# A two-level Strassen run that starts two items sooner in the third column, with one fetch less per item, another order of left forms, and the last results in halves

## The chip, the cores and the metric

The kernel runs on one core of one Trainium2 chip. The metric is the device time of one launch, in microseconds, as the median of several runs. Five engines work side by side, each in its own order: PE multiplies matrices (PEld is its loading of weights), DVE adds tensors, ACT copies and applies tanh, POOL and SP issue transfers from their queues. They wait for one another by semaphores.

## The reference

```python
def reference(a, b, bias):          # a: 4096x4096, b: 4096x4096, bias: 4096, all float32
    return np.tanh(np.matmul(a, b) + bias)
```

## The kernel before

**Tiles.** The output is worked in four columns of 1024 (c = 0 to 3). A row pair is 256 rows; there are 16. One *item* is a row pair in one column, and its work is one level of Strassen-Winograd: seven products instead of eight. The products are named m1 to m7 (`PRODUCTS`); each has a left operand (a quadrant of a such as a11, or a sum such as s2) and a right operand (a quadrant of b such as b11, or a sum such as d3, e6). Each operand is fp16. A whole product is 16 matmuls of 128x512 (line 478, or line 950 within the run described below).

**Two levels.** Two items side by side can be taken together, and a product of both can be split once more: seven products of 8 matmuls of 128x256 (line 889) in place of two whole ones. Their left operands are the *left forms* v1 to v4 (made on DVE into four tiles called h by `left`), besides two halves of the operand itself; their right operands are three quarters of the operand of b and the *right forms* t1 to t4. For m3 and m4 (and for m5 and m7 within a run) the right forms stay in SBUF; `resident` makes those of m5 and m7. For m2 and m6 they are written to DRAM once (`put_four` by way of a staging tile, `put_sum` by two transfers of which the second adds) and pulled again for each pair by `pull_four` on POOL. The five tiles that they are pulled into are blocks of b11 and e6; where another column follows, those blocks are saved in DRAM first (`put_block`) and brought back behind the run.

**Stages of columns 2 and 3.** Each starts with two half items that repeat the row pairs just done (`again`), so that the operands of b can be changed part by part (`change`). Then come pairs of *plain* items, where m3 and m4 go in two levels (`twice_four`) and m2, m5, m1, m6, m7 whole; then the *run*, `four(n)` for each pair, where m2 to m7 go in two levels and only m1 is whole. `FOURS` says how many plain items stand ahead of the run: 4 in column 2, 2 in column 3. The last pair of column 2 *leaves*: its m6 and m7 are whole, since b's operands are restored there for what follows. `turn_over(c)` writes out by hand the last part of the last plain pair and what it loads ahead for the run.

**Order.** The order of every queue is the order in which the program writes the instructions. Time is counted in slots, seven for an item; `at_slot` puts work at a slot. `STAGED`, `ASIDE`, `ADDED`, `SAVED`, `AWAY` and `KEPT_AT` give the slots for forms, counted from the second to last item before the run (slot -14 is the start of the column with two plain items, -28 with four). Lines 250, 258, 371 and 381 are loads of a and b; lines 776, 764, 783 and 790 are the writes of forms and blocks.

**The names that the steps touch.** a12 holds s5, the left operand of m5, and later s7, that of m7. `product` (line 483) fetches a12 of the item two on when it stands in `early_fetch`; `after` (line 573) fetches it when the item is one of a pair. `take_m5` (line 1033) takes the finished m5: it writes o from an output tile (three of them, lines 497 to 498), applies tanh, stores, and takes m5 from ds. Then m7 needs s7 (`asum`) and its v1, and m6 needs its v2. `last` marks the last pair of the program; its end is lines 1200 to 1218. `new_sum` gives a tile for a sum out of a pool of two (`sums`) or, at each third turn, a single spare tile, which the stages use too.

Of the kernel before, what the change touches and what calls it, by code (L numbers as in the profile page):

```python
# [8 lines left out]
P = 128  # L9
QP = 32  # L10
NB = 512
NCW = 2 * NB
# [8 lines left out]
ADD = mybir.AluOpType.add  # L21
# [47 lines left out]

FOUR = ((0, 0), "t1", (1, 0), "t2", "t3", (1, 1), "t4")  # L70
ADDED = {
    2: {("m2", "t3"): (-20, -18)},
    3: {("m2", "t3"): (-12, -10), ("m6", "t3"): (2, 5)},
}
STAGED = {2: (-13, -7, -5, 0, 2, 4, 7), 3: (-8, -6, -4, 1, 4, 7)}
ASIDE = {2: (-9, -10, -6, 2, 4, 5), 3: (-12, -7, -10, -2, 6, 4)}
SAVED = {2: (-13, -8, -13, 5, -5, -7, 5, 7)}
SPARED = (1,)
S6_AT = 2
AWAY = {"m5": -14, "m7": -3}  # L80
# [3 lines left out]
    ("m5", "t1"): -7, ("m5", "t3"): -6, ("m5", "t2"): -3, ("m5", "t4"): -1,  # L84
    ("m7", "t1"): -4, ("m7", "t2"): 0, ("m7", "t4"): 1, ("m7", "t3"): 2,
}
FOURS = {2: 4, 3: 2}

# [34 lines left out]
def kernel(  # L123
# [28 lines left out]
    def tt(out_, in0, in1, op):  # L152
        nc.vector.tensor_tensor(out=out_, in0=in0, in1=in1, op=op)  # L153
# [55 lines left out]
    def beginning(n):  # L209
        return begins.get(items[n][0], len(items))  # L210

    def by_two(n, what):
        return what in twos.get(n, ())

    def again(n):
        return items[n][3]
# [99 lines left out]

    def new_sum(shape, dt, name, n=None):
        pool = sums
        if n is None or not (by_two(n, "m6") or by_two(n - 2, "m6") or n in fours or items[n][0] in FOURS and (not again(n) or items[n][0] == NC - 1 and items[n][2] in SPARED) and n < beginning(n)):
            turns[0] += 1  # L320
            pool = spare if turns[0] % 3 == 0 else sums
        return pool.tile(shape, dt, name=name, tag="sum")
# [667 lines left out]
    def four(n):  # L990
# [17 lines left out]
            at = "w" if what == "m6" else "z"  # L1008
            whole(i, left_, right, ((bank(i, 0, at), ds(0, NB)),), what == "m6", steps)

        def store_half(o, i, j, queue):
            queue.dma_start(
                out=out[ds(2 * pair[i] * P, P), ds(c * NCW + HALF[j].start, HALF[j].size)],
                in_=o[:, HALF[j]],
            )

        def end(name, i, r, j):
            nc.scalar.activation(st[i][name], st[i][name], TANH)
            store(st[i][name], pair[i], r, c, j)
# [13 lines left out]
        def take_m5(i):  # L1033
            st[i]["o"] = new_out()
            tt(st[i]["o"], st[i]["s"], bank(i, 0, "d"), ADD)
            end("o", i, 0, 1)
            tt(st[i]["ds"], st[i]["ds"], bank(i, 0, "d"), SUB)

        def take_m1(i):
# [31 lines left out]
        step(2)  # L1071
        single(n, "m4", 7)
        w2()
        forms_at(1)
        left(n, "m3", "v4")
        u()
        single(n, "m3", 7)
        u2()
        seed(p, "z", 0)
# [48 lines left out]
            fetch(m + 1, "a22")  # L1128
        take_m2(q)
        take_m5(p)  # L1130
        seed(p, "d", 0)
        seed(q, "c", 0)
        asum(q, "s6")
# [5 lines left out]
        one_whole("m1", p)  # L1139
        take_m5(q)  # L1140
        if leave:
            asum(q, "s7")
            take_m1(p)
            if not last:
                fetch(m, "a11")
            for name in ("t1", "t2", "t4"):
                del rights["m5", name], rights["m7", name]
            step(11)
            one_whole("m1", q)
            take_m1(q)  # L1150
            step(12)
            for i in (p, q):
                one_whole("m6", i)
                step(14 if i == p else 16)
                take_m6(i)
                one_whole("m7", i)
                if i == p:
                    fetch(m, "a21")
                    fetch(m, "a12")
                    asum(m, "s2")  # L1160
                take_m7(i)
                step(15 if i == p else 17)
                if i == p:
                    for name in AHEAD[0]:
                        fetch(m + 1, name)
            for name in AHEAD[1]:
                fetch(m + 1, name)
            asum(m, "s5")
            for k in range(18, 29):
                at_slot(SLOTS * m + k - 18, give_back, c, k)  # L1170
            return
        left(n, "m6", "v2")
        group0(n, "m6")
        asum(q, "s7")
        left(n, "m7", "v1")
        take_m1(p)
        if not last:
            fetch(m, "a11")
# [19 lines left out]
        w2()  # L1198
        u()
        if last:  # L1200
            single(n, "m7", 7)
            u2()
            here = bank(q, 0, "d")[:, HALF[0]]
            tt(here, here, st[q]["ds"][:, HALF[0]], SUB)
            o = st[q]["ds"]
            tt(o[:, HALF[1]], o[:, HALF[1]], bank(q, 0, "d")[:, HALF[1]], SUB)
            nc.scalar.activation(o[:, HALF[1]], o[:, HALF[1]], TANH)
            store_half(o, q, 1, nc.sync)
            single(n, "m6", 3)
            take_m6(p)  # L1210
            single(n, "m6", 4)
            take_m6(q)
            single(n, "m7", 3)
            take_m7(p)
            single(n, "m7", 4)
            nc.scalar.activation(o[:, HALF[0]], here, TANH, scale=-1.0)
            store_half(o, q, 0, nc.sync)
            return
        single(n, "m7", 7)
        u2()  # L1220
# [41 lines left out]
    def turn_over(c):  # L1262

        m = begins[c]
        p, q = m - 2, m - 1
        left_count[0] = 0
        del free[:]

        def slot(at):
            for f, args in work.pop(SLOTS * p + at, ()):  # L1270
                if f in (put_four, put_sum, put_block):
                    f(*args)

        queue.extend(
            (what, f) for n in range(m, ends_with[c], 2) for what in ("m2", "m6") for f in FOUR
            if what == "m2" or n + 2 in fours or c == NC - 1
        )
        returned.clear()
        if c < NC - 1:
            returned.append(c)  # L1280
        early_fetch.update((m, m + 1))
        free.extend(("b11_1", "b11_2", "b11_3"))
        for i in range(3):
            pull_four()
        asum(q, "s1")
        asum(q, "s6")
        fetch(m, "a11")
        slot(8)
        product(p, *PRODUCTS[8])
        single(p, "m4", 7)  # L1290
        adds["m4"][1]()
        product(q, *PRODUCTS[2])
        resident_at(-7)
        single(p, "m4", 3)
        twice_after(p, "m4")
        twice_four(p, "m4", 3)
        fetch(m, "a22")
        fetch(m + 1, "a22")
        fetch(m + 1, "a11")
        asum(q, "s7")  # L1300
        slot(9)
        slot(10)
        seed(m, "d", 0)
        resident_at(-6)
        product(q, *PRODUCTS[5])
        fetch(m, "a21")
        slot(12)
        resident_at(-5)
        slot(13)
# [549 lines left out]
```

## Time and profile before

| | us |
|---|---|
| median of three runs | 1522.38 (1521.57 to 1523.24) |
| profiled execution, its own time | 1522.57 |
| its span, first to last instruction | 1520.6 |
| column 2's first product of line 889 | 838.77 |
| column 2's run, first m1 to the m1 of the pair that leaves | 954.46 to 1086.02 |
| column 3's first product of line 889 | 1207.15 |
| column 3's run, first m1 to the end of the span | 1277.02 to 1520.6 |

The granted PE clock is 1.0 throughout. How to read the rows that follow: in a timeline each row has the start, the duration, the engine, the line, the operation with output and inputs, shapes and a count, and in brackets the idle time of that engine ahead of it with what ended it. Rows of the same kind in sequence are merged. In the chain of waits each row is a start, a duration and what the program's end hung on at that time. In a table of windows the columns are the stretch, its length, busy time of PE, PEld, DVE, ACT and POOL (with counts), the clock, the share of the DMA engines and GB/s. A transfer's row ends with its count, size and the median time from issue to landing. DVE's adds all stand on line 153, and the scalar copies of PSUM on lines 895 to 908: both are helpers.

### The profile page before, as it was taken

What the parts mean: (1) busy time and instruction counts of PE and PEld (TensorE: products, weight loads), DVE (VectorE), ACT (ScalarE), POOL (GpSimd) and SP (SyncE); (2) the same over time, 40 slices, a digit from 0 to 9 for tenths busy, and PEclk for the clock granted to TensorE, in tenths of its full rate; (3) what the DMA queues carried; (4) which work ended last, traced back from release to release, by engine and by line L of the source; (5) the groups of instructions that cost most, each with busy time, mean ns of one, the idle gap of its engine ahead of it and who ended that gap; (6) DMA issues with size and microseconds to landing.
All of it is one profiled execution on the core that took longest, in us unless ns stands there. A gap on an engine that the chain in (4) does not pass through costs nothing.

```text
span 1520.6 us, 23784 instructions
## 1 busy us (share of the span) xinstructions
PE 1509.8 (99%) x9005; PEld 878.9 (58%) x9005; DVE 1166.8 (77%) x1619; ACT 377.1 (25%) x809; POOL 479.1 (32%) x868
## 2 busy tenths in 40 slices
PE   9999999999999999999999999999999999999998
PEld 4444444444445566544444557788644467888886
DVE  6789877777876666577787667888658868888887
ACT  4431111111221122111122212333222222333332
POOL 8775543333603231343460220112121121111111
PEclk9999999999999999999999999999999999999999
DMA  9999999999979998999995887898976688888885
GB/s 181 181 217 255 275 247 212 215 214 240 189 212 298 263 278 269 229 258 229 239 188 158 292 293 257 312 344 300 376 247 196 215 284 276 303 311 309 325 332 181
DMA packets 205718, 387.74 MB, mean 255 GB/s; under 512 B 25250, under 2 KB 102306, under 8 KB 205604
## 3 DMA queue, kind: packets, MB, share of 16 engines
q0 software_dynamic: 117232, 198.50, 56.8%
q1 hardware_dynamic: 87844, 187.47, 35.3%
q8 instruction: 70, 1.15, 0.3%
q14 instruction: 44, 0.36, 0.1%
q10 hardware_dynamic: 528, 0.26, 0.1%
HBM read 332.40 MB, written 139.46 MB: 310 GB/s over the span
## 4 chain that ended last, share of the span: by engine, by line
PE 91%; DMA 4%; DVE 3%; POOL 1%; issue 0%; ACT 0%; DVEq 0%; SPq 0%; ACTq 0%; POOLq 0%
PE ps L478 58%; PE ps L889 21%; PE ps L1488 4%; PE ps L950 4%; PE ps L678 4%; DMA a<-scratch 2%; DMA out_dram<-o 1%; DVE h L153 1%; DVE a L153 1%; DVE ps L153 0%; DMA land<-in_a_dram 0%; DVE ds L153 0%; DMA side<-in_b_dram 0%; POOL land L1529 0%; POOL side L1577 0%
## 5 line engine op out<-in xcount | busy, mean ns | idle before, releaser
L478 PEld LDWEIGHTS <-a 128*128 128x128 f16 x3264 | 319.2, 98 | 379.0 <-DMA a<-scratch 0.5
L478 PE MATMUL ps<-b,a 128*128 128x512 f16 x1148 | 262.1, 379 | 0.0
L889 PEld LDWEIGHTS <-h 128*128 128x128 f16 x2048 | 199.2, 98 | 31.8 <-DVE h L153 6.3
L478 PE MATMUL ps<-e,a 128*128 128x512 f16 x932 | 212.1, 379 | 0.0
L478 PE MATMUL ps<-d,a 128*128 128x512 f16 x896 | 202.5, 379 | 0.0
L827 POOL DMA_DIRECT2D form<-form_m x133 | 70.6, 531 | 378.4 <-PE ps L889 337.6
L278 DVE STREAM_TRANSPOSE a<-nat 128x1024 f16<-128x1024 f16 (+2 forms) x202 | 175.2, 911 | 19.1 <-PE ps L478 17.6
L889 PEld LDWEIGHTS <-a 128*128 128x128 f16 x1536 | 150.3, 98 | 24.0
L478 PE MATMUL ps<-d,s 128*128 128x512 f16 x656 | 148.3, 379 | 0.0
L478 PEld LDWEIGHTS <-s 128*128 128x128 f16 x848 | 83.0, 98 | 97.7
L250 POOL DMA_DIRECT2D nat<-in_a_dram x176 | 93.3, 535 | 133.6 <-DVE a L278 64.4
L381 POOL DMA_DIRECT2D b<-in_b_dram x192 | 103.7, 546 | 83.9 <-DVE a L278 30.9
L153 DVE TENSOR_TENSOR a<-a,a 128x2048 f16<-128x2048 f16 (+1 forms) x97 | 116.5, 1201 | 0.2
L153 DVE TENSOR_TENSOR ps<-ps,x 128x256 f32<-128x256 f32 x146 | 60.8, 429 | 60.2 <-ACT x L895 32.8
L889 PE MATMUL ps<-form,h 128*128 128x256 f16 x768 | 98.0, 273 | 2.5 <-DVE h L153 2.5
L502 ACT ACTIVATE o<-ps 128x512 f32<-128x512 f32 x90 | 54.1, 601 | 162.2 <-issue 105.9
L153 DVE TENSOR_TENSOR h<-a,h 128x1024 f16<-128x1024 f16 x128 | 86.7, 684 | 0.0
L889 PE MATMUL ps<-form,a 128*128 128x256 f16 x608 | 77.5, 273 | 0.0
L153 DVE TENSOR_TENSOR ds<-ds,ps 128x512 f32<-128x512 f32 (+1 forms) x94 | 63.6, 678 | 17.3 <-PE ps L889 7.0
L478 PE MATMUL ps<-side,a 128*128 128x512 f16 x288 | 73.9, 379 | 0.0
L950 PE MATMUL ps<-d,a 128*128 128x512 f16 x320 | 72.2, 379 | 0.0
L153 DVE TENSOR_TENSOR h<-a 128x1024 f16<-128x1024 f16 x80 | 54.7, 688 | 16.4 <-DMA a<-scratch 15.7
(187 smaller groups left out, 1874.2 us busy)
## 6 DMA issues: line engine op xcount, KB each, us to landing
a<-scratch SPq DMA_DIRECT2D x144, 512.0 KB, 6.4
form<-form_m POOLq DMA_DIRECT2D x133, 512.0 KB, 5.8
out_dram<-o SPq DMA_DIRECT2D x203, 256.0 KB, 5.5
nat<-in_a_dram POOLq DMA_DIRECT2D x288, 128.0 KB, 6.4
scratch<-a SPq DMA_DIRECT2D x48, 512.0 KB, 6.6
b<-in_b_dram POOLq DMA_DIRECT2D x160, 128.0 KB, 5.5
scratch<-a SPq DMA_DIRECT2D x32, 256.0 KB, 5.7
cast<-in_b_dram POOLq DMA_DIRECT2D x64, 128.0 KB, 10.0
```

Of the source, the lines that this page charges most:

```text
L153: nc.vector.tensor_tensor(out=out_, in0=in0, in1=in1, op=op)
L250: nc.gpsimd.dma_start(out=tl[ds(q * QP, QP), :, :], in_=src.rearrange("(mb p) k -> p mb k", p=QP),)
L278: nc.vector.transpose(dst[:, ds(b0 * tb, n * tb), :].rearrange("P (b t) (mb p) -> P mb b t p", t=tb, p=QP), src[:, :, ds(b0, n), :].rearra ...
L381: nc.gpsimd.dma_start(out=dst[ds(q * QP, QP), ds(t, nt)], in_=src)
L478: nc.tensor.matmul(st[where], at, bt, start=(what == "m2" or n < LEAD and what == "m1") and i == 0, stop=i == len(ts_) - 1, skip_group_che ...
L502: nc.scalar.activation(o, src, TANH)
L678: nc.tensor.matmul(to, at, bt, start=False, stop=t == TP - 1, skip_group_check=True)
L827: nc.gpsimd.dma_start(out=rights[what, name], in_=forms[what, name])
L889: nc.tensor.matmul(to, at, bt, start=False, stop=t == TP - 1, skip_group_check=True)
L950: nc.tensor.matmul(to[:, half], at[:, t // TB, t % TB], bop[right, t // TB][:, t % TB, half], start=anew and t == 0, stop=t == T - 1, skip ...
L1488: nc.tensor.matmul(mb[m % 4, j], aq[m, kt // T][:, kt % T, :], right(kt, j), start=fresh and kt == k0, stop=stop and kt == k1 - 1, skip_gr ...
```

## The change

Four edits.

1. **The run of column 2 starts two items sooner** (`FOURS` 4 to 2): items 33 and 34 go from the plain kind into the run, which then has five pairs in column 2 instead of four; column 3 has six in both. The slots of the forms of column 2 become those of column 3; m6's t3 is made by adding transfers there too; the saved blocks have new slots; and s1 of the second repeated item of column 2 takes the pool of two, as column 3's does.
2. **No second fetch of a12**: `turn_over` no longer puts the first two items of the run into `early_fetch`, so that line 483 doesn't fetch what line 573 fetches.
3. **Order in the run**: s7 and m7's v1 go ahead of m6's v2 and its first products; taking m5 from ds (`less_m5`) is its own step, and for the second item it goes behind them. One group of resident forms (m7's t4) is made behind m3's v4 and its add instead of ahead.
4. **The last pair**: m6 and m7 of the last item are both finished in halves, the second half of the columns first; the order of the last four products is m6, m7 of the first item, then m6, m7 of the second; the very last store goes out from ACT's queue.

```diff
 ADDED = {
-    2: {("m2", "t3"): (-20, -18)},
+    2: {("m2", "t3"): (-12, -10), ("m6", "t3"): (2, 5)},
...
-STAGED = {2: (-13, -7, -5, 0, 2, 4, 7), 3: (-8, -6, -4, 1, 4, 7)}
-ASIDE = {2: (-9, -10, -6, 2, 4, 5), 3: (-12, -7, -10, -2, 6, 4)}
-SAVED = {2: (-13, -8, -13, 5, -5, -7, 5, 7)}
+STAGED = {2: (-8, -6, -4, 1, 4, 7), 3: (-8, -6, -4, 1, 4, 7)}
+ASIDE = {2: (-12, -7, -10, -2, 6, 4), 3: (-12, -7, -10, -2, 6, 4)}
+SAVED = {2: (-16, -15, -11, -9, -14, -13, 0, 3)}
...
-FOURS = {2: 4, 3: 2}
+FOURS = {2: 2, 3: 2}
...
-  ... items[n][0] in FOURS and (not again(n) or items[n][0] == NC - 1 and items[n][2] in SPARED) and n < beginning(n)
+  ... items[n][0] in FOURS and (not again(n) or items[n][2] in SPARED) and n < beginning(n)
...
             end("o", i, 0, 1)
+
+        def less_m5(i):
             tt(st[i]["ds"], st[i]["ds"], bank(i, 0, "d"), SUB)
...
         w2()
-        forms_at(1)
         left(n, "m3", "v4")
         u()
+        forms_at(1)
...
         take_m5(p)
+        less_m5(p)
...
         take_m5(q)
         if leave:
+            less_m5(q)
...
+        asum(q, "s7")
+        left(n, "m7", "v1")
         left(n, "m6", "v2")
         group0(n, "m6")
-        asum(q, "s7")
-        left(n, "m7", "v1")
+        less_m5(q)
         take_m1(p)
...
         if last:
+            parts = {"m6": ("s", "w", ADD, 1.0, 1), "m7": ("ds", "d", SUB, -1.0, 0)}
+
+            def first_half(what):
+                name, at, op, scale, r = parts[what]
+                o, here = st[q][name], bank(q, 0, at)
+                tt(here[:, HALF[0]], here[:, HALF[0]], o[:, HALF[0]], op)
+                tt(o[:, HALF[1]], o[:, HALF[1]], here[:, HALF[1]], op)
+                nc.scalar.activation(o[:, HALF[1]], o[:, HALF[1]], TANH)
+                store_half(o, q, r, 1, nc.sync)
+
+            first_half("m6")
             single(n, "m7", 7)
             u2()
-            here = bank(q, 0, "d")[:, HALF[0]]
-            tt(here, here, st[q]["ds"][:, HALF[0]], SUB)
-            o = st[q]["ds"]
-            tt(o[:, HALF[1]], o[:, HALF[1]], bank(q, 0, "d")[:, HALF[1]], SUB)
-            nc.scalar.activation(o[:, HALF[1]], o[:, HALF[1]], TANH)
-            store_half(o, q, 1, nc.sync)
+            first_half("m7")
             single(n, "m6", 3)
             take_m6(p)
-            single(n, "m6", 4)
-            take_m6(q)
             single(n, "m7", 3)
             take_m7(p)
-            single(n, "m7", 4)
-            nc.scalar.activation(o[:, HALF[0]], here, TANH, scale=-1.0)
-            store_half(o, q, 0, nc.sync)
+            for what in ("m6", "m7"):
+                name, at, op, scale, r = parts[what]
+                single(n, what, 4)
+                o = st[q][name]
+                nc.scalar.activation(o[:, HALF[0]], bank(q, 0, at)[:, HALF[0]], TANH, scale=scale)
+                store_half(o, q, r, 0, nc.sync if what == "m6" else nc.scalar)
             return
...
-        early_fetch.update((m, m + 1))
```

More of the change, by code (lines that the diff above doesn't have):

```diff
@@ L318, in new_sum @@
         pool = sums
-        if n is None or not (by_two(n, "m6") or by_two(n - 2, "m6") or n in fours or items[n][0] in FOURS and (not again(n) or items[n][0] == NC - 1 and items[n][2] in SPARED) and n < beginning(n)):
+        if n is None or not (by_two(n, "m6") or by_two(n - 2, "m6") or n in fours or items[n][0] in FOURS and (not again(n) or items[n][2] in SPARED) and n < beginning(n)):
             turns[0] += 1
@@ L1009, in one_whole, with store_half @@
             whole(i, left_, right, ((bank(i, 0, at), ds(0, NB)),), what == "m6", steps)
-        def store_half(o, i, j, queue):
+        def store_half(o, i, r, j, queue):
             queue.dma_start(
-                out=out[ds(2 * pair[i] * P, P), ds(c * NCW + HALF[j].start, HALF[j].size)],
+                out=out[ds((2 * pair[i] + r) * P, P), ds(c * NCW + r * NB + HALF[j].start, HALF[j].size)],
                 in_=o[:, HALF[j]],
```

## The prediction

> **What bounds the kernel now.** I read the page first, then who waited for whom on the matmul engine, then the chain of waits and the timelines of PE, DVE and SP around each gap.
>
> ```profile
> span 1520.6 us, 23784 instructions
> PE 1509.8 (99%) x9005; PEld 878.9 (58%) x9005; DVE 1166.8 (77%) x1619; ACT 377.1 (25%) x809; POOL 479.1 (32%) x868
> PE ps L889 <- DVE h L153: 3.5, 7, 0.9
> ```
>
> PE is busy for all but 10.8 us, and behind the start it waits for one thing only: seven times for a left form (h) from DVE. So two things can move the time: fewer matmul microseconds, and gaps in PE. Everything else matters only when it makes PE wait, or behind the last matmul.
>
> **Matmul time removed.** Two items of the plain kind (m3 and m4 in two levels, the rest whole) against two items of the run in two levels, in the chain of waits:
>
> ```profile
> 838.77 1.75 PE ps L889 x16
> ...
> 885.53 1.75 PE ps L889 x16
> ...
> 998.27 3.45 PE ps L950 x16
> ...
> 1041.86 3.45 PE ps L950 x16
> ```
>
> The rows 838.77 and 885.53 are the same place of two successive plain pairs: 46.76 us. The rows 998.27 and 1041.86 are m1 of two successive pairs of the run: 43.59 us. Counted: a whole product is 16 matmuls in 3.45 us; a form's product is 8 in 0.873 us (1.75 for 16). m2, m5, m6 and m7 go from 8 x 3.454 = 27.6 us to 28 x 0.873 = 24.5 us, which is the same 3.17 us. The diff moves one pair of column 2 (items 33 and 34) from the first kind to the second; the pair that leaves the run stays as it is. **Minus 3.17 us.** The bounds are narrow (3.1 to 3.2), since neither kind shows a gap in its steady part. The new pair pulls fourteen more forms through POOL and stores what it did before; the steady pairs of the run pull as many in the same 43.59 us, so that traffic is hidden as theirs is.
>
> **Gaps in PE at the start of each run.** The matmul records overlap (273 ns long, one each 109 ns), so an idle time shown as 0.87 is a loss of more: the start of the group less the start of the one before it, less 0.873 us for its eight.
>
> ```profile
> 1264.46 1.04 PE L889 MATMUL ps<-b,a 128*128 128x256 f16 x8
> 1266.37 1.05 PE L889 MATMUL ps<-form,h 128*128 128x256 f16 x8 [0.87 <-DVE h L153]
> ...
> 1271.62 1.04 PE L889 MATMUL ps<-b,h 128*128 128x256 f16 x8
> 1273.24 1.05 PE L889 MATMUL ps<-form,h 128*128 128x256 f16 x8 [0.59 <-DVE h L153]
> ```
>
> ```profile
> 938.28 1.04 PE L889 MATMUL ps<-g,a 128*128 128x256 f16 x8
> 939.36 1.03 PE L889 MATMUL ps<-d,h 128*128 128x256 f16 x8
> ...
> 949.06 1.04 PE L889 MATMUL ps<-b,h 128*128 128x256 f16 x8
> 950.68 1.05 PE L889 MATMUL ps<-form,h 128*128 128x256 f16 x8 [0.59 <-DVE h L153]
> ```
>
> Column 3: 1266.37 - 1264.46 - 0.87 = 1.04, and 0.75 at 1273.24. Column 2: 0.75 at 950.68. Worked out the same way, gaps too short for the waits table add 0.21 at 939.36 (0.20 at its twin in column 3) and, in each column, two or three of 0.08 to 0.18, about 0.3 together. Sum: 1.3 us in column 2, 2.2 us in column 3. What they wait for, from the chain (two rows) and DVE's timeline:
>
> ```profile
> 1252.19 8.83 DMA a<-scratch
> 1261.04 4.56 DMA a<-scratch
> ```
>
> ```profile
> 943.06 0.69 DVE L153 TENSOR_TENSOR h<-a 128x1024 f16<-128x1024 f16 x1 [1.64 <-DMA a<-scratch]
> ...
> 1265.62 0.69 DVE L153 TENSOR_TENSOR h<-a 128x1024 f16<-128x1024 f16 x1 [2.58 <-DMA a<-scratch]
> ```
>
> The h at 1265.62 is m5's v1, made from s5, which lies in a12 of the second item. That tile is fetched twice, one behind the other: SP holds the second until the first has landed (1261.02), and it lands at 1265.6. The first copy is the one line 573 still issues. With it alone DVE, free at 1263.04 (1265.62 less 2.58), makes v1 at once; it ends at 1263.7 and PE needs it at 1265.33. Everything behind it on DVE, v4 of m2 at 1273.24 among it, comes 2.58 us sooner (1.64 in column 2); it was 0.75 late, and PE now reaches it some 1.2 us sooner (0.3 in column 2), so it is still in time, by 0.6 in both. The short gap at 939.36 is m3's fourth left form and its add, queued behind m7's t4 (two DVE instructions of 0.64 each); the diff lets the forms step pass behind them, 1.28 us against 0.21. Each SP queue also loses two transfers of 512 KB per column, with the wait between them, so what stands behind (the stores, a21) is issued sooner, not later. **Minus 3.5 us**, bounds 0 (the first copy turns out late as well) and 3.5.
>
> Column 2's new start of the run has the slots of column 3's present one, less the second fetch, so I take no gap for it either.
>
> **The gap ahead of m7's first form product.**
>
> ```profile
> 1374.25 1.05 PE L889 MATMUL ps<-side,h 128*128 128x256 f16 x8 [0.33 <-DVE h L153]
> ...
> 1461.98 1.05 PE L889 MATMUL ps<-side,h 128*128 128x256 f16 x8 [0.36 <-DVE h L153]
> ...
> 1504.70 1.04 PE L889 MATMUL ps<-e,a 128*128 128x256 f16 x8
> 1506.11 1.05 PE L889 MATMUL ps<-side,h 128*128 128x256 f16 x8 [0.36 <-DVE h L153]
> ```
>
> ```profile
> 1502.30 0.69 DVE L153 TENSOR_TENSOR o<-s,ps 128x512 f32<-128x512 f32 x1 [0.94 <-DMA out_dram<-o]
> 1502.90 0.68 DVE L153 TENSOR_TENSOR ds<-ds,ps 128x512 f32<-128x512 f32 x1
> 1503.50 0.69 DVE L153 TENSOR_TENSOR h<-a,h 128x1024 f16<-128x1024 f16 x1
> ...
> 1505.36 0.69 DVE L153 TENSOR_TENSOR h<-a 128x1024 f16<-128x1024 f16 x1
> ```
>
> take_m5 of the second item waits for an output buffer until its store has landed, just ahead of 1502.30; behind it on DVE stand ds, m6's v2, s7 and only then m7's v1. Losses by the same reckoning: 0.49, 0.52, 0.54, together 1.5 us. The diff puts ds and m6's v2 behind m7's v1: 2 x 0.60 = 1.2 us sooner, more than each loss. What is late next is m6's v2: it ends at about 1505.3 and PE uses it two products behind m7's v1, at 1507; ds is needed by less_m1 only, later on DVE still. **Minus 1.5 us**, bounds 0 and 1.5.
>
> One more gap stays, in the pair that leaves column 2, which the diff keeps as it is:
>
> ```profile
> 1073.62 1.05 PE L889 MATMUL ps<-form,h 128*128 128x256 f16 x8 [0.41 <-DVE h L153]
> ```
>
> **The end.** Behind the last matmul:
>
> ```profile
> 1514.22 1.28 DVE L153 TENSOR_TENSOR s<-s,ps 128x512 f32<-128x512 f32 x2
> ...
> 1514.85 1.04 PE L889 MATMUL ps<-form,a 128*128 128x256 f16 x8
> ...
> 1516.13 0.63 ACT L1018 ACTIVATE ds<-ds 128x512 f32<-128x512 f32 x1
> 1516.67 0.37 ACT L1216 ACTIVATE ds<-ps 128x256 f32<-128x256 f32 x1
> ...
> 1517.21 0.41 SPq L1012 DMA_DIRECT2D out_dram<-ds  x1
> ```
>
> ```profile
> out_dram<-ds SPq DMA_DIRECT2D x1, 128.0 KB, 2.2
> ```
>
> Last matmul 1515.9, last activation 1517.04, last store issued 1517.21, landed 1519.4, span's end 1520.6. The end is a queue on DVE and ACT, not PE's last product. The diff replaces one of the s adds (0.60) by two half adds (about 0.8), all before take_m7, so take_m7's add and activation come 0 to 0.2 us later; behind them ACT now has two half activations (0.37 each) instead of one, the last ending about 1517.4. Its store is issued from ACT's own queue at once, about 1517.45, and takes the 2.2 us of the row, since a half and 256 KB go out just before it, as they do now. **Plus 0.2 us**; bounds -0.9 (both halves slip in ahead of take_m7's, and the last starts as PE ends) and +0.5 (DVE's extra 0.2 comes on top).
>
> A rule bears on that queue. The Trainium skill, "DMA: Bandwidth & Descriptors", section "Issuing engines are not separate DMA queues", says that transfers from any engine share the same 16 DMA engines, and that another issuer saves only the time of issuing. By it the store gains nothing but SP's issue, and the term stays +0.2; were the queue a path of its own, the end would come out about even.
>
> **The entry of column 2.** The saved blocks, stages and copies that fill the forms move to the column's first slots, and three of the blocks come ahead of the last raw b loads (b21) on POOL, which works in order. What that costs, no row shows.
>
> ```profile
> 770.00:780.00 10.00, 10.00 (x48) 4.57 (x47) 6.88 (x8) 3.59 (x7) 6.16 (x12) 1.00 1.16 202
> ```
>
> ```profile
> 780.69 4.12 POOL L381 DMA_DIRECT2D b<-in_b_dram x7 [0.37 <-DMA b<-in_b_dram]
> ```
>
> ```profile
> 799.14 3.49 DVE L153 TENSOR_TENSOR d<-b,b 128x2048 f16<-128x2048 f16 x3
> 806.07 0.70 DVE L153 TENSOR_TENSOR ps<-ps,aside 128x512 f32<-128x512 f32 x1 [3.44 <-PE ps L478]
> ```
>
> ```profile
> b<-in_b_dram POOLq DMA_DIRECT2D x160, 128.0 KB, 5.5
> ...
> side<-block_e POOLq DMA_DIRECT2D x2, 512.0 KB, 10.6
> ```
>
> Block 2 of b21 is issued by 782.9 (the fourth of seven), lands about 788.4, and DVE needs it for d4 at 800.28: 11.9 us to spare, then DVE's 3.44 us of idle time less 1.3 us for the stage that now comes ahead (two adds of the h kind): 14.0 us before PE can feel it. Three saved blocks of 0.524 MB go in front: at the 202 GB/s of this stretch 7.8 us, plus 1.8 us of issuing (4.12 / 7 each). That is under the 14.0 us, and costs nothing; the upper bound is the slowest 512 KB row, 10.6 us each one after another, 31.8 us, a stall of 17.8. I take nothing, as the rate of the stretch itself is the nearer row. m6's t3 of column 2 is now made by adding transfers: two DVE adds fewer, POOL transfers in their place, as column 3 has them. The sums condition sends s1 of column 2's second repeated item to the pool of two and leaves the spare tile to the stages, as in column 3; by the count of turns s1 of column 3's first repeated item then takes the spare tile, and the first stage there waits for that item's m1. DVE waits for m1's neighbours at that place anyway, so I price it at nothing; uncovered it would be part of a product, under 3.45 us of DVE, with the same 3.44 us of idle time behind it.
>
> **Sum**, against the profiled execution's own 1522.57 us (span 1520.6 and 2.0 around it; the median shown is 1522.38, 0.2 less): -3.17 - 3.5 - 1.5 + 0.2 = -8.0. From the median: **1514.4 us**, its own range 1513.6 to 1515.8.
>
> **Rivals.**
> A. The wait ahead of m7's first form is handed on: m6's v2 or a later left form, now behind it on DVE (77% busy), comes late. In the three pairs that have the gap today: 1514.4 + 1.5 = 1515.9; in all ten pairs of the two runs at 0.52 each: 1519.6. For it: DVE is behind every gap of the waits table. Against: v2 has 1.6 us.
> B. The second fetch isn't what m5's v1 waits for: the first copy, or the DMA engines behind it, is as late without it. Then the 3.5 us at the run starts stay, and column 2 takes column 3's 2.2 for its own 1.3: 1514.4 + 3.5 + 0.9 = 1518.8. Against: the chain's two rows end within 0.1 us of the second's start and of DVE's.
> C. Slower. The saved blocks, ahead of b21 on POOL, are served one after another at 10.6 us each; d4 is 17.8 us late past its cover, DVE stands, and PE with it: 1514.4 + 17.8 = 1532. It is felt from 14.0 / 3 = 4.7 us a block, and slower than before from (14.0 + 8.0) / 3 = 7.3. For it: the DMA share of 1.16 there. Against: at that share it moved 202 GB/s, 2.6 us a block.
>
> **How the numbers follow.** Forecast 0.64, A 0.14, B 0.16, C 0.06. The range, 1513.2 to 1518.2, holds the forecast, A but for its far end and B where part of the fetch's effect stays; the rest of B and C lie outside. What a measurement of this kernel can tell from no change is 0.2%, 3.0 us: faster is below 1519.3. The forecast, most of A and most of B are: 0.87; their far ends within: 0.07; C slower: 0.06.
>
> **What would show it.** Right: in column 2, 28 form products (224 matmuls on line 889) more and 8 whole ones (128 on line 478) fewer; one a12 fetch per item; no wait of PE for h at the run starts and ahead of m7's first form; the gap of the leaving pair still there. Wrong: d4's adds waiting for b21 at column 2's entry, an h of m6 late instead of m7's, or the last activation beyond 1517.4 counted from a last matmul at 1515.9.

## The result and the profile after

The changed kernel takes **1526.88 us** (1524.58 to 1527.44), the kernel before, in the same comparison, 1522.41 (1519.94 to 1526.18): ratio 1.0024, 95% interval 1.0015 to 1.0034. It is slower by 4.5 us, where 1514.4 was forecast. The profiled execution has 1526.86 us of its own and a span of 1525.1, against 1522.57 and 1520.6, so its spans differ by the same 4.5 us and can be taken apart.

The head of the page after, and the view of who waited for whom on PE (us in total, times, longest):

```profile
span 1525.1 us, 24074 instructions
PE 1508.3 (99%) x9101; PEld 890.1 (58%) x9101; DVE 1180.3 (77%) x1646; ACT 383.6 (25%) x830; POOL 488.4 (32%) x885
```

```profile
PE ps L478 <- DVE ps L153: 5.8, 1, 5.8
PE ps L889 <- DVE ps L153: 1.9, 4, 1.0
PE ps L950 <- DMA e<-block_e: 1.6, 1, 1.6
...
PE ps L889 <- DVE h L153: 0.5, 1, 0.5
```

PE has 96 matmuls more (224 of 128x256 for 128 of 128x512) and 1.5 us less busy time. The seven waits for h (3.5 us) are down to one, and three waits that the kernel before did not have are there instead. Where in the program they fall, the chain of waits after tells:

```profile
846.58 1.75 PE ps L889 x16
...
914.34 3.45 PE ps L950 x16
...
957.93 3.45 PE ps L950 x16
...
1212.28 1.75 PE ps L889 x16
...
1280.04 3.45 PE ps L950 x16
```

Set against the marks of before in the table above:

| stretch | before, us | after, us | difference |
|---|---|---|---|
| start to column 2's first product of line 889 | 838.77 | 846.58 | +7.81 |
| from there to column 3's first | 368.38 | 365.70 | -2.68 |
| from there to the first m1 of column 3's run | 69.87 | 67.76 | -2.11 |
| from there to the span's end | 243.58 | 245.06 | +1.48 |

The second row holds three things: the moved pair's -3.17 (957.93 - 914.34 = 43.59 against 46.76), -1.17 at the run's start (914.34 - 846.58 = 67.76, against 954.46 - 838.77 = 115.69 less the 46.76 of the moved pair), and +1.66 in the rest of the run, the pair that leaves and the exit. The largest part of the 1.66 is the pair that leaves, where PE waits 1.6 us for a saved block of e6 instead of 0.41 us for a left form; the prediction took that pair as unchanged. The first row stands out. (The two executions differ by another 0.49 us in column 0, where the diff changes nothing: it comes out at 99.50 instead of 99.99. So the entry of column 2 costs 8.3.)

**The entry of column 2.** PE and DVE at the place, after:

```profile
813.94 3.62 PE L478 MATMUL ps<-e,a 128*128 128x512 f16 x16
823.40 5.92 PE L478 MATMUL ps<-d,a 128*128 128x512 f16 x16 [5.84 <-DVE ps L153]
829.15 3.62 PE L478 MATMUL ps<-d,s 128*128 128x512 f16 x16
```

```profile
799.91 0.69 DVE L153 TENSOR_TENSOR stage<-side 128x1024 f16<-128x1024 f16 x1
800.51 0.69 DVE L153 TENSOR_TENSOR stage<-b 128x1024 f16<-128x1024 f16 x1
...
809.64 1.22 DVE L153 TENSOR_TENSOR d<-b,b 128x2048 f16<-128x2048 f16 x1
819.17 1.29 DVE L153 TENSOR_TENSOR stage<-stage,b 128x1024 f16<-128x1024 f16 x2 [8.31 <-DMA form_m<-stage]
...
822.65 1.29 DVE L153 TENSOR_TENSOR ps<-ps,s 128x512 f32<-128x512 f32 x2
```

PE stands 5.84 us for the adds on PSUM (the tiles ps that PE writes) that start at 822.65, and these wait in DVE's order behind m2's t2, which DVE could not begin for 8.31 us. t2 is made in place over t1 in the one staging tile, so it may not start until t1 has been read out to DRAM. d4's adds, which the prediction watched, were done by 803.5, so the loads of b21 were in time. Why was t1 read out so late? POOL's timeline, after:

```profile
798.60 0.55 POOL L790 DMA_DIRECT2D block_b<-b  x1
802.51 1.33 POOL L783 DMA_DIRECT2D form_m<-b  x1 [3.36 <-DMA form_m<-side]
...
806.50 1.07 POOL L790 DMA_DIRECT2D block_b<-b  x1
807.04 1.07 POOL L776 DMA_DIRECT2D form_m<-stage  x1
```

t1 was ready at 801.1 and was issued at 807.04: POOL itself was waiting 3.36 us for the first of two transfers of `put_sum` to land before it could issue the one that adds, and quarters and a saved block stood ahead too. Then it took 12.03 us to land (the chain has it from 807.04 to 819.08), against 5.5 us for the median of its kind, at a DMA share of 1.10. The same stretch, before and after (length, PE, PEld, DVE, ACT, POOL, clock, DMA share, GB/s):

```profile
807.00:819.00 12.00, 12.00 (x58) 5.42 (x56) 11.03 (x14) 2.37 (x4) 0.00 (x0) 1.00 0.48 136
```

```profile
807.00:819.00 12.00, 10.56 (x49) 4.70 (x48) 3.56 (x4) 2.37 (x4) 2.61 (x5) 1.00 1.10 326
```

Before, t1's stage was made 34 us later:

```profile
834.38 0.69 DVE L153 TENSOR_TENSOR stage<-side 128x1024 f16<-128x1024 f16 x1
```

Behind PE's stand come another 2.5 us: the 96 matmuls from 823.40 to 846.58 take 23.18 us, and at 3.454 us for 16 they should take 20.7. (By starts, as the prediction reckons, the stand is 6.0 us, 823.40 - 813.94 - 3.454, and the slow matmuls 2.3; the sum stays 8.3.) The last section returns to that.

**The gap ahead of m7.** It is gone from m7's first form but for one pair, and stands at m7's third product instead (number 3 in `single`, made with v4), where PE waits for an add of DVE (`u()` in the program) into the same part of PSUM. Second pair of column 3's run, DVE and PE:

```profile
1331.01 0.69 DVE L153 TENSOR_TENSOR o<-s,ps 128x512 f32<-128x512 f32 x1 [2.24 <-DMA out_dram<-o]
...
1332.87 0.69 DVE L153 TENSOR_TENSOR h<-a 128x1024 f16<-128x1024 f16 x1
...
1341.33 0.76 DVE L153 TENSOR_TENSOR ps<-ps,x 128x256 f32<-128x256 f32 x2 [0.49 <-ACT x L895]
```

```profile
1341.82 1.03 PE L889 MATMUL ps<-e,h 128*128 128x256 f16 x8 [1.04 <-DVE ps L153]
```

From m7's v1 to that add DVE needs 8.46 us (1341.33 - 1332.87). (The 0.49 us of idle time ahead of the add, for a copy by ACT, stands there in the kernel before too.) Before, it was 7.26, in the corresponding pair (1336.61 - 1329.35) as in the last, where the prediction shows v1 at 1505.36 and the chain of waits has the add:

```profile
1512.62 0.78 DVE ps L153 x2
```

The two instructions moved behind v1 (2 x 0.60) are exactly the difference. DVE is behind from the moment the output buffer comes free, and stays behind; the change only moved the place where PE runs into it.

### The profile page after: what moved, and what is told of

Its sections match the earlier page's. It is cut to its first block, busy times and chain, and to the rows that moved or that the text cites. A ratio compares the mean times of both kernels' runs of the same rounds, so it can differ in the third digit from the quotient of the medians.

```text
span 1525.1 us, 24074 instructions
## 1 busy us (share of the span) xinstructions
PE 1508.3 (99%) x9101; PEld 890.1 (58%) x9101; DVE 1180.3 (77%) x1646; ACT 383.6 (25%) x830; POOL 488.4 (32%) x885
## 3 DMA queue, kind: packets, MB, share of 16 engines
q8 instruction: 71, 1.16, 0.3%
## 4 chain that ended last, share of the span: by engine, by line
PE 86%; DMA 6%; DVE 5%; issue 1%; POOL 1%; ACT 1%; SPq 0%; DVEq 0%; ACTq 0%; POOLq 0%
PE ps L478 52%; PE ps L889 21%; PE ps L1499 5%; PE ps L678 4%; PE ps L950 3%; DMA out_dram<-o 2%; DVE h L153 2%; DVE ps L153 1%; DMA b<-in_b_dram 1%; DVE a L153 1%; DVE ds L153 1%; DMA form_m<-stage 1%; DVE s L153 1%; POOL b L381 1%; DMA e<-block_e 1%
## 5 line engine op out<-in xcount | busy, mean ns | idle before, releaser
L478 PEld LDWEIGHTS <-a 128*128 128x128 f16 x3136 | 307.3, 98 | 372.6 <-issue 9.2
L478 PE MATMUL ps<-b,a 128*128 128x512 f16 x1092 | 249.2, 379 | 0.0
L889 PEld LDWEIGHTS <-h 128*128 128x128 f16 x2176 | 212.8, 98 | 29.5 <-issue 2.9
L478 PE MATMUL ps<-d,a 128*128 128x512 f16 x896 | 204.8, 382 | 5.8 <-DVE ps L153 5.8
L827 POOL DMA_DIRECT2D form<-form_m x147 | 77.8, 529 | 413.5 <-PE ps L889 372.2
L478 PE MATMUL ps<-e,a 128*128 128x512 f16 x876 | 199.4, 379 | 0.0
L889 PEld LDWEIGHTS <-a 128*128 128x128 f16 x1632 | 159.6, 98 | 24.8 <-issue 0.3
L478 PE MATMUL ps<-d,s 128*128 128x512 f16 x624 | 141.0, 379 | 0.0
L153 DVE TENSOR_TENSOR a<-a,a 128x2048 f16<-128x2048 f16 (+1 forms) x103 | 123.9, 1204 | 0.2
L889 PE MATMUL ps<-form,h 128*128 128x256 f16 x848 | 108.1, 273 | 0.0
L889 PE MATMUL ps<-form,a 128*128 128x256 f16 x672 | 85.6, 273 | 0.1
L950 PE MATMUL ps<-d,a 128*128 128x512 f16 x352 | 79.4, 379 | 0.0
L950 PEld LDWEIGHTS <-a 128*128 128x128 f16 x416 | 40.7, 98 | 46.3 <-issue 1.8
```

The source lines that it names most:

```text
L478: nc.tensor.matmul(st[where], at, bt, start=(what == "m2" or n < LEAD and what == "m1") and i == 0, stop=i == len(ts_) - 1, skip_group_che ...
L827: nc.gpsimd.dma_start(out=rights[what, name], in_=forms[what, name])
L889: nc.tensor.matmul(to, at, bt, start=False, stop=t == TP - 1, skip_group_check=True)
L950: nc.tensor.matmul(to[:, half], at[:, t // TB, t % TB], bop[right, t // TB][:, t % TB, half], start=anew and t == 0, stop=t == T - 1, skip ...
```

## The experiments

The theories, as the expectations number them. **Theory 1:** the entry's loss is t1's transfer, issued late on POOL's queue and landing at full DMA engines, so that DVE waits for the staging tile. **Theory 3:** the pair gaps are DVE's whole queue behind the wait of `take_m5` for an output buffer, not the order of the left forms. What is set against them stands in the expectations. Except where a diff is against the kernel before, it is against the changed kernel; each ratio is to the kernel before on the same chip.

**Stages later** (`a_late_stages`). m2's t2 and t4, and the first stage of m6, go into later slots; t1 and everything else stay.

```diff
-STAGED = {2: (-8, -6, -4, 1, 4, 7), ...
+STAGED = {2: (-8, -2, 0, 2, 4, 7), ...
```

> The changed kernel, with m2's t2 and t4 of column 2 staged six slots later (slots -2 and 0 in place of -6 and -4, m6's t1 at 2); every transfer stays. Theory 1 (the staging tile: t2 overwrites t1's tile and DVE waits for t1's transfer, which is issued late on POOL): t1's transfer has landed by then, the PE gap of 5.84 us at column 2's entry and the 2.5 us at half clock behind it go, and the first product of line 889 in column 2 starts at about 838.3 instead of 846.4; the time is 8.3 us shorter, about 1518.6. Theory 2 (the DMA engines are too full at the entry, whatever the order): DVE waits for another transfer there, b21 or the later stage, and a gap of some us stays; 1522 to 1526.

Measured: 1518.42 us (1515.57 to 1521.21), ratio 0.9975 (0.9965 to 0.9985). The entry is whole again, by the chain of waits:

```profile
838.67 1.75 PE ps L889 x16
```

That is 7.9 us sooner than after. t1 is hardly sooner: it is issued at 805.30, and DVE takes the stage up again only at 823.87, without a wait. The loss was the wait for the tile, and nothing else that the earlier start puts on POOL stops PE at the entry.

**Only t1's transfer on another queue** (`d_t1_on_sp`). The slots stay; t1 of m2 is issued by SP, in both columns.

```diff
-        nc.gpsimd.dma_start(out=forms[what, name], in_=staged[what, name])
+        queue_ = nc.sync if (what, name) == ("m2", "t1") else nc.gpsimd
+        queue_.dma_start(out=forms[what, name], in_=staged[what, name])
```

> The changed kernel with the transfer of m2's t1 from the staging tile on SP's queue instead of POOL's, in both columns; everything else stays, DMA bytes too. Theory 1: it is issued right behind the stage (about 801 instead of 807), lands before DVE comes to t2 at 810.8 or up to 3 us later, and the PE gap goes or is under 1 us: about 1518.6 to 1519.5. Theory 2: the transfer takes as long to land on full engines wherever it is issued (12 us, to 813 and more), and PE's gap shrinks by less than half: 1523 or more.

Measured: 1518.75 us (1517.09 to 1521.72), ratio 0.9978 (0.9969 to 0.9986). SP and DVE in this run:

```profile
801.68 0.33 SPq L777 DMA_DIRECT2D form_m<-stage  x1
```

```profile
811.35 1.29 DVE L153 TENSOR_TENSOR stage<-stage,b 128x1024 f16<-128x1024 f16 x2 [0.23 <-DMA form_m<-stage]
...
823.95 1.29 DVE L153 TENSOR_TENSOR stage<-b,stage 128x1024 f16<-128x1024 f16 x2 [5.51 <-DMA form_m<-stage]
```

Issued 5.4 us sooner, t1 still takes some 9.6 us to land, but it is there when DVE wants it. The wait has not quite gone: t4 now waits 5.51 us for t2's turn of the tile, and PE does not feel it there. So most of it is the time of issue: t1 lands 7.8 us sooner, 5.4 by its issue and 2.4 by a shorter way, with the DMA share still at 1.04 from 802 to 811. That the way takes 9.6 to 12 us there, against the median of 5.5, is theory 2's part of the loss; it alone does not stop PE.

**POOL cleared ahead of t1** (`b_pool_clear`). Saved blocks, quarters and sums go behind; the stages keep their slots.

```diff
-    2: {("m2", "t3"): (-12, -10), ("m6", "t3"): (2, 5)},
+    2: {("m2", "t3"): (-3, 0), ("m6", "t3"): (2, 5)},
...
-ASIDE = {2: (-12, -7, -10, -2, 6, 4), ...
-SAVED = {2: (-16, -15, -11, -9, -14, -13, 0, 3)}
+ASIDE = {2: (-3, -1, -2, -2, 6, 4), ...
+SAVED = {2: (-3, -1, 0, 5, -2, 1, 5, 7)}
```

> The changed kernel, stages where they are; the saved blocks, the quarters and the first two adding transfers of column 2 come behind slot -4 on POOL, so that only t1, t2 and t4 stand there from -8 to -4. Same bytes in all, moved some 30 us later. Theory 1: t1's transfer is issued about 801 instead of 807 and lands within 6 us, DVE's wait shrinks from 8.3 us to under 2 and PE has no gap: about 1518.6. Theory 2: the same result if the load is only shifted, so this one tells only that POOL's order or load matters; against both, a gap that stays at 5.8 us would put the fault on DVE's own amount of work. A new wait may open where the blocks are taken for the run (about 900).

Measured: 1530.99 us (1527.24 to 1532.45), ratio 1.0051 (1.0036 to 1.0065), so the expected time was missed by far. At the place it did what was expected: t1 is issued at 802.09, t2 starts at 811.50 without a wait. But the same wait comes back for m6's t2, 40 us later, where the postponed blocks and sums now lie:

```profile
841.54 0.55 POOL L776 DMA_DIRECT2D form_m<-stage  x1 [1.51 <-DMA form_m<-e]
```

```profile
857.97 1.29 DVE L153 TENSOR_TENSOR stage<-stage,e 128x1024 f16<-128x1024 f16 x2 [8.53 <-DMA form_m<-stage]
```

PE stands 10.13 us there. The mechanism is confirmed at a second place; the remedy is to keep the stage's transfers apart from the rest, not to push the rest along.

**The run's start as before** (`c_start_as_before`). Edit 1 undone, edits 2 to 4 kept.

```diff
-FOURS = {2: 2, 3: 2}
+FOURS = {2: 4, 3: 2}
...
```

(with it `ADDED`, `STAGED`, `ASIDE`, `SAVED` of column 2 and the condition on sums, as before)

> The changed kernel with column 2's run starting where it did before (its slots, FOURS and the sums condition as before); the single fetch of a12, the order of left forms and the halves at the end stay. If the entry and the pair that leaves are the only costs of starting sooner: no PE gap at 820, the leaving pair's 1.7 us wait for a block of e6 gone, 3.2 us more matmul time: 1526.9 - 8.3 - 1.7 + 3.2 = 1520.1. The run starts of both columns stay free of gaps (3.5 us won against before); the later pairs show gaps ahead of m7's third product, 1 to 2 us together. If the second fetch or the order of forms is to blame for the slower time, it stays above 1522.4.

Measured: 1521.28 us (1518.51 to 1525.47), ratio 0.9992 (0.9982 to 1.0002). As expected the run starts show no gap and the wait for the block of e6 is gone; the gaps ahead of m7's third product sum to 2.7 us by starts, more than the 1 to 2. What matters is the distance to the run with later stages, 0.9992 to 0.9975, some 2.6 us: that is what edit 1 brings once the entry is mended. Both ratios are uncertain by 0.1%, so this agrees with the 3.17 of the matmuls but doesn't measure it closely.

**One fetch alone** (`j_before_one_fetch`). The kernel before with edit 2 only.

```diff
-        early_fetch.update((m, m + 1))
```

> The kernel before with one change, the second fetch of a12 left out. If the second fetch alone is what m5's v1 waits for at the run starts: the gaps of 1.0 and 0.75 us in column 3 and 0.75 in column 2 go, and most of the small ones with them, 2.5 to 3.5 us: 1519.2. If the first copy is as late, or the change in place of m7's t4 is what did it: 1521.5 or more, with the gaps in the profile.

Measured: 1520.66 us (1517.95 to 1523.41), ratio 0.9982 (0.9973 to 0.9991), 2.7 us. The run starts have no gap left but one of 0.2 in each column (ahead of m3's fourth left form, which edit 3 removes). But m7's first form is now later than before, in this profile 4.9 us by starts over five pairs against 1.5 over three; two of them:

```profile
1417.64 1.05 PE L889 MATMUL ps<-side,h 128*128 128x256 f16 x8 [0.89 <-DVE h L153]
...
1462.36 1.05 PE L889 MATMUL ps<-side,h 128*128 128x256 f16 x8 [0.96 <-DVE h L153]
```

Its profiled execution was the slowest of its runs, so this sum is an upper one. The direction is still worth noting: no order of DVE was touched, and yet a later wait has grown.

**The order of left forms as before** (`f_order_before`), on the run with later stages.

```diff
+        less_m5(q)
...
-        asum(q, "s7")
-        left(n, "m7", "v1")
         left(n, "m6", "v2")
         group0(n, "m6")
-        less_m5(q)
+        asum(q, "s7")
+        left(n, "m7", "v1")
```

> The kernel with the late stages and the order of left forms of the kernel before: m6's v2 and the subtraction of m5 ahead of s7 and m7's v1. Theory 3: DVE does the same work up to u in either order, so u is as late and what was a gap ahead of m7's third product is in part one ahead of m7's first; the sum over the pairs stays within 1 us of the 6.4 of the late stages, 1518 either way. Theory 4, or if the new order itself makes the gaps: the gaps ahead of m7's third product go and only three short ones ahead of its first stay (1.5 us in all): about 1514.

Measured: 1518.43 us (1517.14 to 1521.02), ratio 0.9975 (0.9966 to 0.9984), against 1518.42 and 0.9975 with the new order. The gaps are at m7's first form again (0.16 to 0.60 in seven pairs, 3.0 us) and none at its third product. The view of waits puts four of them down to a copy by ACT (line 901). v1's add ends within 0.1 us of that copy each time (at the first of the four 1004.39 against 1004.44), so the name decides nothing between theories 3 and 4; the next run does. The order is worth nothing that these runs can tell (0.1% either way).

**take_m5 behind the left forms** (`e_m5_later`), also with later stages. What waits for the output buffer goes behind s7 and the two left forms.

```diff
-        take_m5(q)
         if leave:
+            take_m5(q)
             less_m5(q)
...
         asum(q, "s7")
         left(n, "m7", "v1")
         left(n, "m6", "v2")
+        take_m5(q)
         group0(n, "m6")
```

> The kernel with the late stages, and take_m5 of the second item, which waits for an output buffer's store, put behind s7, m7's v1 and m6's v2 on DVE. Theory 3 (in the pairs of the run DVE's whole queue from that wait to m7's add, u, is the bound; the wait passes on to whatever PE needs next): the wait of 1.2 to 3.0 us is then covered by 2.4 us of work that doesn't need the buffer, the gaps ahead of m7's third product (0.1 to 1.2 us, 5.0 in all with the profile of the late stages) and of its first (1.4) shrink to under 0.5 in all but a pair or two: about 1514 to 1515. Theory 4 (the gaps come from a later landing of forms or from ACT's copies, not from DVE's order): the gaps stay, 1518.

Measured: 1515.47 us (1514.39 to 1516.94), ratio 0.9953 (0.9941 to 0.9965). The waits of PE in this run that lie in the pairs, the pair that leaves (one of the two for h, and the block of e6) and the exit (a's transfer):

```profile
PE ps L478 <- DMA a<-scratch: 0.6, 1, 0.6
PE ps L889 <- DVE h L153: 0.5, 2, 0.3
...
PE ps L950 <- DMA e<-block_e: 0.4, 1, 0.4
```

None is left for u. Against the run with later stages (4.1 us in five waits for u and 1.2 for h, in a profile that was the slowest of its runs) nearly all of that is gone, for 3 us. Theory 3 holds: the wait has to leave the place ahead of the left forms; shuffling what is behind it does not help. (Its five runs lie within 2.6 us, the eleven with later stages within 5.6; that shows no smaller spread, since the five of `g_end_before`, without this edit, lie within 1.6.)

**The end as before**, alone (`g_end_before`) and with take_m5 later (`h_m5_later_end_before`). Edit 4 is undone in both:

```diff
-            parts = {"m6": ("s", "w", ADD, 1.0, 1), "m7": ("ds", "d", SUB, -1.0, 0)}
...
+            single(n, "m6", 4)
+            take_m6(q)
             single(n, "m7", 3)
             take_m7(p)
-            for what in ("m6", "m7"):
...
+            single(n, "m7", 4)
+            nc.scalar.activation(o[:, HALF[0]], here, TANH, scale=-1.0)
+            store_half(o, q, 0, 0, nc.sync)
```

> The kernel with the late stages and the end of the kernel before (whole m6 results, m6's products ahead of m7's, the last store from SP). From the first product of m6's last three to the end of the span: 10.7 us with the halves in the changed kernel, 10.1 in the kernel before; if the halves cost what these two show, 0.6 us less, about 1517.8, which the times can hardly tell but the profile's end can. If the halves pay, the end is later by 0.3 or more.

> Late stages, take_m5 later and the end of the kernel before together: by theory 3 the sum of the three, 1513.5, faster than the kernel before by some 8.5 us; by theory 4 about 1517.8.

Measured: 1517.15 us (1516.37 to 1517.94), ratio 0.9963 (0.9951 to 0.9975), for the first. Its time proves little, as the pair gaps differ from run to run by as much; its profile's end contradicts the 10.1 that was expected. From the start of m6's product with v3 in the last pair to the end of the span it is 1516.1 - 1505.13 = 10.97 us, where the run with later stages and halves has 1519.4 - 1508.91 = 10.49. By the sign that was set the halves pay there. DVE is behind at the end of this profile, and PE waits for it ahead of the last product:

```profile
1509.92 1.03 PE L889 MATMUL ps<-form,a 128*128 128x256 f16 x8 [0.22 <-DVE ds L153]
```

The second is the clean pair with `e_m5_later`, without the pair gaps: 1514.81 us (1514.20 to 1515.16), ratio 0.9948 (0.9936 to 0.9960), 1.3 above what was expected. Here the same stretch is 1512.4 - 1502.48 = 9.92 us with the end of before and 1513.7 - 1503.12 = 10.58 with halves, and the medians differ by the same 0.66, though their intervals overlap. So the halves cost some 0.7 us where DVE is in time; where it is behind, the one profile without them has the longer end. What they cost in general stays open. **This version has the lowest median of all**, 8.3 us under the kernel before in its call. Its page:

```profile
span 1512.4 us, 24062 instructions
PE 1504.8 (99%) x9101; PEld 889.6 (59%) x9101; DVE 1180.1 (78%) x1645; ACT 383.0 (25%) x829; POOL 488.9 (32%) x885
```

**The pair that leaves** (`i_leave_order`), on the fastest version: m6 reads the e6 block that comes back last at the end of its sum, and a21 is fetched ahead of the stores.

```diff
-                one_whole("m6", i)
+                one_whole("m6", i, (*range(4), *range(8, 15), *range(4, 8), 15))
                 step(14 if i == p else 16)
+                if i == p:
+                    fetch(m, "a21")
                 take_m6(i)
```

> Late stages, take_m5 later, the end of the kernel before, and in the pair that leaves column 2: m6 of the leaving items takes block 1 of e6, which lands last, behind blocks 2 and 3, and a21 of the next item is fetched ahead of the store of m6's result on SP instead of behind it. The wait for the block (0.1 to 1.7 us in the runs with the sooner start) and the 0.7 us gap at the exit should go: 1514.8 less 0.8 to 1.2, 1513.8; if the DMA engines, full there, set the landing whatever the order, the exit's gap stays and it is 1514.5.

Measured: 1515.69 us (1514.87 to 1515.86), ratio 0.9948 (0.9934 to 0.9961): nothing gained. In its profile the wait at the exit is longer, not shorter (0.97 shown, 0.57 without the edit), and a second one stands behind it that the version without the edit doesn't have:

```profile
1102.90 1.04 PE L478 MATMUL ps<-side,a 128*128 128x512 f16 x4 [0.97 <-DMA a<-scratch]
...
1108.78 1.89 PE L478 MATMUL ps<-b,a 128*128 128x512 f16 x8 [0.52 <-DVE s L153]
```

The edit explains the second: the store of m6's result, now behind a21 on SP, is issued at 1099.26 instead of 1095.95, and DVE waits 0.77 us for it ahead of that sum, where it waited 0.28.

**Edit 1 once more** (`k_i_start_as_before`): that version with the run's start as before, the same edit as above.

> i_leave_order with column 2's run starting where it did before. With every wait that the sooner start brought taken away from both, the difference is the matmul time of one pair: 3.2 us, 1517.0 where i_leave_order has 1513.8. A difference under 2 would say that the sooner start still costs something else at column 2's entry.

Measured: 1516.59 us (1515.72 to 1517.21), ratio 0.9955 (0.9943 to 0.9968), so edit 1 brings 0.9 us by the medians and 1.3 by the spans (1515.2 to 1513.9), where 3.2 were expected; the two intervals overlap. The m1 of the same pair of column 2 and the first m1 of column 3's run, first in this run and then with edit 1:

```profile
1040.21 3.45 PE ps L950 x16
...
1273.89 3.45 PE ps L950 x16
```

```profile
1036.94 3.45 PE ps L950 x16
...
1271.77 3.45 PE ps L950 x16
```

3.27 us sooner while the run lasts, as the matmuls say; 2.12 by column 3's run. The 1.15 between is lost in the pair that leaves and at the exit. There PE waits 1.0 us for a21's transfer and 0.5 for a sum with edit 1, and 0.6 for a sum without. Why they differ isn't settled.

## Why the prediction was wrong

**The step that failed is "The entry of column 2"**, the price of nothing for it. It cost 8.3 us, 5.84 as a stand of PE and 2.5 as slow matmuls behind it. The prediction asked which saved blocks stand ahead of b21 on POOL, and followed b21 to d4. That part holds: the last raw load of b is issued some 7 us later (794.51, against about 787.6 before), which is within the cover of 14.0. It did not ask the same of the other thing on that queue that DVE waits for: the staging tile, of which there is one, filled again and again, each time behind the transfer that empties it. The diff brought t1 from the column's slot 15 to slot 6 and t2 from 21 to 8, in among blocks, quarters and adding transfers, and the 14.0 us of cover belonged to another chain. Rival C had the right queue, but named the wrong item, and priced it as late blocks (17.8). The rate it argued from, 202 GB/s at a share of 1.16, was no reserve either: at a share of 1.10 one 512 KB transfer took 12.03 us to land. Later slots for the stages behind t1, or t1 alone on SP, give 1518.4 and 1518.8 and settle it.

**"The gap ahead of m7's first form product", minus 1.5, fell too**, and rival A's mechanism held, though at an add and not at m6's v2 or another left form. The losses that stood at the first form, 1.5 us in three pairs, became 3.4 in six places, five of them at the third product (by starts: 0.24, 0.52, 0.63 at a first form, 1.20, 0.49, 0.36). The step looked at one instruction and its neighbours; DVE had no slack up to that add, so what went behind v1 came out late by its own 1.2 us. The two orders measured equal. What helped is the wait's place (3 us).

**"The end", plus 0.2**: from m6's product with v3 to the span's end it grew by 0.59 (10.12 to 10.71), and by 0.66 in the clean pair, just beyond the upper bound of 0.5; with DVE behind it went the other way (10.97 without halves, 10.49 with). The last activation did end later, 1.32 us behind the last matmul against 1.15; the rest is 0.3 ahead of the last matmul, in which PE's last product was held up, and a longer way from the last issue to the end (3.66 us from ACT's queue, 3.39 from SP's).

**What was right.** Matmul time: -3.17, and -3.17 measured between two pairs. The gaps at the run's starts: -3.5 predicted, -1.17 and -2.11 measured; the second fetch was the cause, and the edit alone brings 2.7 us (rival B falls). It concerned the first two items of each run and not every item, as the title has it: the transfers from scratch to a go from 144 to 140. The sum over the edits, by ratios to the kernel before: edit 2 -0.18% (uncertain by 0.09%), and by differences of two ratios, uncertain by about 0.14%: edits 3 and 4 +0.10%, edit 1 with its stages later -0.17%, the stages' slots +0.49%. So that edits 3 and 4 cost time is not shown by the times.

That the forecast of 1514.4 is close to what the fastest version measures, 1514.81, is luck: it gets there by another route, with later stages, take_m5 later and no halves.

## What to carry to other kernels

- When work is moved earlier, list each buffer that is filled more than once along it, and for each fill the transfer that must have emptied it: when it is issued on its queue (count what stands ahead, and the waits of the queue itself), and how long it takes at the load of that stretch.
- DVE, working in its order, started late after one wait and stayed late up to the add that PE needed. Find such a wait and move it; exchanging the work behind it only moved the gap here.
- A stall removed is worth its size only if nothing downstream is nearly late: of the 3.27 us that edit 1 won in the last comparison, 2.12 were left when column 3's run began.

## What the runs showed of the hardware

**A stand of PE costs more than its length.** The granted clock fell within the idle time at the entry, and came back only some time after work had resumed (windows of 1 us, after; the last three columns are the clock, the DMA share and GB/s):

```profile
820.00:821.00 1.00, 0.00 (x0) 0.00 (x0) 1.00 (x2) 0.00 (x0) 0.24 (x1) 1.00 1.13 353
821.00:822.00 1.00, 0.00 (x0) 0.00 (x0) 1.00 (x2) 0.00 (x0) 0.31 (x1) 0.63 1.09 401
822.00:823.00 1.00, 0.00 (x0) 0.00 (x0) 1.00 (x2) 0.00 (x0) 0.00 (x0) 0.50 1.04 357
...
827.00:828.00 1.00, 1.00 (x3) 0.29 (x2) 1.00 (x2) 1.00 (x2) 0.13 (x1) 0.50 0.00 0
828.00:829.00 1.00, 1.00 (x6) 0.48 (x5) 1.00 (x3) 0.09 (x1) 1.00 (x2) 0.96 0.03 12
```

PE is idle from 817.56 (813.94 + 3.62); a mean of 0.63 puts the fall at 821.26, after 3.7 us, and 0.96 the return at 828.08, 4.7 us after work resumed at 823.40. In the run with POOL cleared it is 3.2 us (850.73 to 853.92) and 3.3 us (860.86 to 864.16):

```profile
853.00:854.00 1.00, 0.00 (x0) 0.00 (x0) 0.00 (x0) 0.00 (x0) 0.00 (x0) 0.96 1.12 366
...
864.00:865.00 1.00, 1.00 (x11) 0.87 (x9) 1.00 (x2) 0.47 (x2) 1.00 (x4) 0.92 0.93 50
```

The gaps of 1.0 and 1.6 us ahead of 1341.82 and 1098.78 left the clock at 1.0. The Trainium skill, "TensorE: Matmul & The Clock Gate", section "What's actually happening", says that the clock halves after an idle window of about 3.4 us and returns after about as much of sustained work, and that the window runs free of the program. The trace agrees for 3.2 and 3.7 us to the fall and for one return, 3.3 us; the other, 4.7 us, is 1.3 us longer than that figure, and no run here shows the window itself. At a clock of 0.5, 4.7 us of work lose 2.3 us, which are the slow matmuls of the entry counted by starts. So a stand of 5.84 us cost 8.3.
